# Fifteen weight slabs of block 2 split early and kept in DRAM as two parts, latent products among the gate products, full-height score products, and squares added on VectorE

## The chip, the cores and the metric

The kernel runs on one core of a Trainium2 chip. The metric is the device time of one execution in microseconds (us); lower is better. The core has five engines that run their own instruction queues in order: TensorE (PE, with its weight loads as PEld), VectorE (DVE), ScalarE (ACT), GpSimd (POOL) and SyncE (SP). SP issues most transfers; POOL issues some.

## The reference

1024 tokens of width 1024 pass through two blocks, in float32.

```python
# block 1
mod = silu(c) @ w_ada + b_ada                    # six vectors: shift, scale, gate, twice
h = rms_norm(x, g_pre_mix) * (1 + scale1) + shift1
xin, b_gate, c_gate, q, k, v, g = split(h @ w_in)            # 7 x 512 columns
y = concat(short_conv(xin, b_gate, c_gate), retention(q, k, v, g))
x = x + gate1 * rms_norm(y @ w_out, g_post_mix)
h = rms_norm(x, g_pre_mlp) * (1 + scale2) + shift2
x = x + gate2 * rms_norm(square(relu(h @ w_fc1)) @ w_fc2, g_post_mlp)
# block 2
a_q, a_k, a_v, i_q, i_k, i_w, c_q, c_kv, k_r, g = split(rmsnorm(x) @ w_in_2)
# indexer, 4 heads of 64: score = sum_h i_w * relu(i_q . i_k / 8); the top 256 keys of each query
# DSA: 8 heads of 64, one shared key/value head, attention over the selected keys, with a position bias
y_a = softmax(a_q . a_k / 8 + bias, over the selected keys) @ a_v
# MLA: latents c_q (256) and c_kv (128), each normalised and projected up; 8 heads of 64 + 32 (rotary)
y_b = softmax(causal (q_nope . k_nope + q_rope . k_rope) / sqrt(96)) @ v_b
gates = sigmoid(g + b_gate)                                   # 2 x 1024
x = x + (gates[0] * (y_a @ w_branch_a) + gates[1] * (y_b @ w_branch_b)) @ w_out_2
x = rmsnorm(x + square(relu(rmsnorm(x) @ w_ff1)) @ w_ff2, final_norm_g)
```

## The kernel before

**Precision.** Each float32 operand is held as two parts: a high part rounded to the short format that TensorE multiplies at full speed, and a low part, the rest. A product is three matmuls: high x high, high x low, low x high. A "unit" is one output tile of 128 features by 512 tokens (one half H of the tokens) over a contraction of 1024: 8 k-tiles x 3 = 24 matmuls of 128x512 (`unit`). Activations lie transposed, features on the partitions, so the weights are the stationary operand.

**Weights.** A `Stream` carries the weights in slabs of 128x1024 (512 KB). For each slab SP loads it into one of three raw tiles `wr`; ScalarE rounds it into the high tile `wh`; VectorE (or GpSimd, where `lo_engine` is set to it) subtracts to give the low tile `wl`. There are three split slots; `next()` hands out a slab and starts the split of slabs ahead. The list of slabs is written down in advance, in order of use, by `plan1` (block 1) and `plan2` (block 2).

**Order of work.** The main line issues units in a written order. Beside it, `Background` keeps lanes of generators (normalisations, retention steps, index scores, selection). A `tick` after each group of matmuls takes each lane one step on; a step yields a number of ticks to rest, a tuple of tiles that must have been written by a modelled clock (`Clock`), or "vector". The attention part is instead put in order by a planner (`Plan`) that knows a modelled cost for each step.

**Stages (us of the profiled execution).** Block 1's normalisation and first products to 195; the rest of its in-projection in four parts with the retention steps as a background lane, 195 to 427; out-projection of both halves (`out_proj`) 427 to 520; MLP up 520 to 857 (`up_first`, then `up_rest`), down to 1172. Block 2's projection: for each half of the tokens 12 units (`NZ` = 12: two of index queries, one `z2` with index keys, rotary keys and index weights, nine of gates), 1195 to 1365, with index scores beside them; then gate features m = 9 to 15 for both halves at once (1365 to 1446, 11.2 us each); then `bias_spread`, one transfer on POOL's queue that spreads the position-bias table within DRAM into `biasd` (4 MB); then six latent units (c_q twice, c_kv, for each half, 1446 to 1482) whose results are normalised by `latents` in the background; then ten units of DSA keys/values and queries. The selection of the top 256 (`top_k`) runs in the background on VectorE and ScalarE from 1340 to 1575. MLA follows to 1741, DSA to 1926, then the branches, `out2` and the second MLP.

**Slab order from the gates on (`plan2`).** Gate slabs m = 9 to 15 (seven), then three latent slabs twice (once for each half), then five key/query slabs twice: 23 loads and splits. From the second half's `z2` on `lo_engine` is GpSimd.

**Score products.** A query tile holds the high parts of 64 query features on partitions 0 to 63 and the low parts on 64 to 127. The key tile (`ik` for the indexer, `ak` for DSA) holds the high key parts on both halves of the partitions, and the low key parts on partitions 0 to 63 only, in further columns. One score tile is two matmuls: all 128 rows against the high keys, then 64 rows (high queries) against the low keys. DSA adds a mask matmul with the identity for query blocks from 2 on.

```python
nc.tensor.matmul(p[:, :w], self.iqs[:, s], self.ik[:, c0:c0 + w], start=True, stop=False)
nc.tensor.matmul(p[:, :w], self.iqs[0:64, s], self.ik[0:64, D + c0:D + c0 + w],
                 start=False, stop=True)
```

MLA's score products have 96 rows (64 + 32 features).

**Squares.** `sq_add` squares a tile on ScalarE and adds it to a running sum, on GpSimd unless another engine is given. `ada_chunks` streams the 12 column chunks of w_ada on POOL's queue in pairs of k-tiles and accumulates them on VectorE; it yields 3 ticks before it uses each.

Of the kernel before, what the change touches and what calls it, by code (L numbers as in the profile page):

```python
# [11 lines left out]
F32 = mybir.dt.float32  # L12
F32R = mybir.dt.float32r
BF16 = mybir.dt.bfloat16
I32 = mybir.dt.int32
AF = mybir.ActivationFunctionType
# [3 lines left out]
P = 128  # L20
T = 512
D = 1024
# [21 lines left out]
NZ = 12  # L44
# [299 lines left out]
class Stream:  # L344
# [42 lines left out]
    def add(self, width, pieces):  # L387
        x = {}

        def load():  # L390
            raw = x["raw"] = self.raw_tile()
            for dst, src in pieces:
                self.m.nc.sync.dma_start(dst(raw), src)

        after = self.ring("wr", self.RAW, len(self.entries))
        self.entry(self.parts_of(lambda: x["raw"][:, :width], width), load, after)

# [83 lines left out]
class Model:  # L481
# [321 lines left out]
    def ada_chunks(self, chunks, st):  # L803


        nc = self.nc
# [12 lines left out]
        for i, (c, k) in enumerate(todo):  # L819
            if k == 0:  # L820
                acc = self.t2()
            s = st[i % 2]
            yield 3
# [279 lines left out]
    def out_proj(self, x, nk=8):  # L1103

        f, acc = self.U(), self.acc_tile()
        for m in range(8):
            w = self.ws.next()
            p = self.ps()
            self.unit(p, w, x, nk)
            s = slice(m * T, m * T + T)  # L1110
            self.nc.scalar.activation(f[:, s], p, AF.Copy)
            self.sq_add(acc, f[:, s], m == 0)
        return f, acc
# [416 lines left out]
    def block1(self):  # L1530
# [109 lines left out]
        gD = bg.add(ada_rest(), lane=2)  # L1640
        ret = bg.add(self.retention(q, k, v))
# [9 lines left out]
        for part in range(4):  # L1651
# [5 lines left out]
            for m in range(4):  # L1657
                w = ws.next()
                p = self.pd()
                self.unit(p[:, 0], w, hA)  # L1660
                self.unit(p[:, 1], w, hB)
                pf = p.rearrange("p a b -> p (a b)")
# [14 lines left out]
                else:  # L1677
# [4 lines left out]
                    self.mix_part(mix[0], q, 1, m, 0)  # L1682
        bg.finish()
# [27 lines left out]
        bg.add(chain_b(f, acc))  # L1711
        self.up_first(hs[0])
# [192 lines left out]
    def plan2(self):  # L1905
# [3 lines left out]

# [14 lines left out]
        for m in range(NZ - 3, 16):  # L1924
            s.cols(w, GT + m * P)
        for cs in ((CQ, CQ + P, CKV), (AK, AQ, AQ + P, AQ + 2 * P, AQ + 3 * P)):
            for _ in range(2):
                for c in cs:
                    s.cols(w, c)
# [21 lines left out]
        self.plan_mlp(a["w_ff1_2"], a["w_ff2_2"])  # L1951

# [14 lines left out]
    def z_evac(self, kind, m, H, p):  # L1967
# [8 lines left out]
        elif kind == "z2":  # L1976
# [5 lines left out]
            nc.vector.tensor_sub(self.ik[0:64, lo], zr[0:64], self.ik[0:64, c].bitcast(F32))  # L1982
            return zr
# [51 lines left out]
    def index_scores(self, qbs, per=1):  # L2035
        nc = self.nc
        n_done = 0
        for qb in qbs:
            sc = self.score_tile(qb)
            n = P * (qb + 1)  # L2040
            for c0 in range(0, n, T):
                w = min(T, n - c0)
                for h in range(4):
# [3 lines left out]
                    nc.tensor.matmul(p[:, :w], self.iqs[0:64, s], self.ik[0:64, D + c0:D + c0 + w],  # L2047
                                     start=False, stop=True)
# [188 lines left out]
    def z_phase(self, xs, hs, f, acc, G2):  # L2237
# [19 lines left out]
        for H in range(2):  # L2257
            if H == 1:
                bg.finish(g0)
            for i in range(NZ):  # L2260
# [9 lines left out]
                if kind == "z2":  # L2270
# [9 lines left out]
                    else:  # L2280
# [10 lines left out]
                        bg.add(topk())  # L2291
        for m in range(NZ - 3, 16):
# [5 lines left out]
        bg.finish(scores)  # L2298
        self.bias_spread()
        self.lat = self.pair()  # L2300
        for H in range(2):
            raws = [self.t2(), self.t2()]
            raws.append(self.rope[:, 3 * D + H * T:3 * D + H * T + T])
            for m in range(3):
                w = ws.next()
                p = self.ps()
                self.unit(p, w, hs[H])
                nc.scalar.activation(raws[m], p, AF.Copy)
            bg.add(self.latents(raws, H), lane=1)
# [78 lines left out]
    def front(self, t, n, p, qb, marks):  # L2388
# [27 lines left out]
        a = step("PE", 1.3e-3 * w + 0.06, t, scores, self.inputs[n] + [self.last_a], takes=("pd",))  # L2416
# [141 lines left out]
    def qk_dsa(self, h, qb, lp):  # L2558
# [4 lines left out]
        for c0 in range(0, n, T):  # L2563
            w = min(T, n - c0)
            nc.tensor.matmul(lp[:, c0:c0 + w], q[:, qs], self.ak[:, c0:c0 + w], start=True, stop=False)
            nc.tensor.matmul(lp[:, c0:c0 + w], q[0:64, qs], self.ak[0:64, D + c0:D + c0 + w],
# [203 lines left out]
    def dsa_begin(self):  # L2770
# [20 lines left out]

        def turn():
# [18 lines left out]
        c = step("Pool", 2.4, t + 3, low, [b[0]])  # L2811
        d = step("PE", 0.6, t + 4, turn, [a], takes=("ps",))
# [88 lines left out]
    def out2(self, x, h, H):  # L2901
# [3 lines left out]
        for m in range(8):  # L2905
# [6 lines left out]
            self.sq_add(acc, x[:, s], m == 0)  # L2912
# [133 lines left out]
    def run(self):  # L3046
# [3 lines left out]
        self.xtokd = self.dp.tile([P, 2, 4 * D], F32, name="xtokd")  # L3050
        self.plan1()
# [38 lines left out]
```

## Time and profile before

| | us |
|---|---|
| median of 3 runs | 2787.26 (2783.12 to 2792.57) |
| profiled execution | 2785.2 |
| its span | 2783.4 |
| mean granted TensorE clock in it | 0.979 |
| TensorE busy | 2656.4 |
| VectorE busy | 1891.4 |
| ScalarE busy | 1334.7 |
| GpSimd busy | 439.1 |

The span is the time from the first to the last instruction that the profiler saw. Busy times are sums over an engine's instructions. Because one wrapper issues every instruction, all of them carry the same line, L183, and are told apart by the names of their tiles: `ps` and `pd` are PSUM tiles, `u` large activation tiles, `t` small ones, `wr`, `wh` and `wl` the raw, high and low weight tiles, `topk` the selection's. A line of the trace reads: engine, operation, output <- inputs, then shapes (for a matmul rows*columns of its stationary operand, then rows x columns of the moving one), type and count.

### The profile page before, as it was taken

The numbers are of one execution on the slowest core, as the hardware profiler recorded it, in microseconds if no ns is written. First come the engines' busy times: TensorE is split into PE (matmuls) and PEld (weight loads), VectorE is DVE, ScalarE is ACT, GpSimd is POOL, SyncE is SP. The second block draws the span as 40 slices with busy tenths as digits, with TensorE's granted clock in tenths as the row PEclk, the third lists the DMA queues.
The fourth block names the chain that finished last, engine by engine and source line by source line (L and its number), as shares of the span: only waits on it lengthen the run. The fifth ranks groups of instructions, "written<-read, shape, count | busy, mean of one in ns | idle before, by whom it ended". The sixth has DMA issues, their size and how long they took to land.

```text
span 2783.4 us, 33424 instructions
## 1 busy us (share of the span) xinstructions
PE 2656.4 (95%) x12052; PEld 2097.2 (75%) x12052; DVE 1891.4 (68%) x3155; ACT 1334.7 (48%) x2182; POOL 439.1 (16%) x384
## 2 busy tenths in 40 slices
PE   5999999999999999899998899999999999999987
PEld 4777777767888887776776678777887788888866
DVE  6573566777665567776898888786557466646656
ACT  4651114465444443444685477875135554443333
POOL 5040102300000110001223411420121000002012
PEclk7999999999999999999999999999999999999999
DMA  6542336454545896743334201453454564459773
GB/s 203 177 130 83 102 110 197 130 174 134 152 125 195 251 226 194 197 135 89 83 107 148 75 16 39 145 153 106 151 160 158 178 217 145 149 196 274 189 207 124
DMA packets 361708, 419.21 MB, mean 151 GB/s; under 512 B 33205, under 2 KB 265572, under 8 KB 360516
## 3 DMA queue, kind: packets, MB, share of 16 engines
q1 hardware_dynamic: 330664, 304.77, 35.4%
q0 software_dynamic: 30544, 112.14, 14.6%
q8 instruction: 95, 1.56, 0.2%
q14 instruction: 73, 0.60, 0.1%
q10 hardware_dynamic: 332, 0.14, 0.0%
HBM read 339.68 MB, written 80.45 MB: 151 GB/s over the span
## 4 chain that ended last, share of the span: by engine, by line
PE 61%; DVE 9%; ACT 6%; DMA 4%; issue 2%; POOL 0%; ACTq 0%; SPq 0%; POOLq 0%; DVEq 0%
PE ps L183 44%; PE pd L183 17%; DVE u L183 4%; ACT u L183 4%; DMA t<-opd 3%; DVE t L183 3%; ACT t L183 1%; DVE topk L183 1%; ACT wh L183 1%; DVE wl L183 1%; DVE tiny L183 1%; DMA opd<-t 0%; DMA wr<-in_w_in 0%; POOL wl L183 0%; POOL t L183 0%
## 5 line engine op out<-in xcount | busy, mean ns | idle before, releaser
L183 PE MATMUL ps<-u,wh 128*128 128x512 f32 (+1 forms) x3568 | 1146.8, 402 | 17.5 <-ACT wh L183 9.1
L183 PEld LDWEIGHTS ps<-u,wh 128*128 128x128 f32 (+1 forms) x3568 | 670.4, 190 | 189.5 <-ACT wh L183 13.1
L183 PE MATMUL ps<-u,wl 128*128 128x512 f32 (+1 forms) x1784 | 713.4, 400 | 7.6 <-DVE wl L183 5.9
L183 PE MATMUL pd<-u,wh 128*128 128x512 f32 x1600 | 521.5, 407 | 7.9 <-ACT u L183 5.5
L183 PEld LDWEIGHTS ps<-u,wl 128*128 128x128 f32 (+1 forms) x1784 | 339.1, 190 | 96.6 <-DVE wl L183 11.9
L183 DVE TENSOR_TENSOR wl<-wr,wh 128x1024 fp32r<-128x1024 f32 (+3 forms) x209 | 238.4, 1147 | 199.8 <-ACT wh L183 195.1
L183 PEld LDWEIGHTS pd<-u,wh 128*128 128x128 f32 x1600 | 299.0, 190 | 84.6 <-ACT u L183 6.4
L183 PE MATMUL pd<-u,wl 128*128 128x512 f32 x800 | 317.7, 397 | 0.0
L183 ACT ACTIVATE wh<-wr 128x1024 fp32r<-128x1024 f32 (+3 forms) x244 | 225.8, 931 | 177.7 <-PE pd L183 83.9
L183 ACT ACTIVATE t<-ps 128x512 f32<-128x512 f32 (+5 forms) x339 | 173.6, 522 | 237.5 <-PE ps L183 228.7
L183 DVE TENSOR_TENSOR t<-ps,t 128x384 fp32r<-128x384 f32 (+3 forms) x354 | 192.5, 563 | 91.8 <-PE ps L183 61.1
L183 ACT ACTIVATE u<-t 128x512 fp32r<-128x512 f32 (+4 forms) x174 | 145.2, 837 | 185.2 <-DVE t L183 117.2
L183 ACT ACTIVATE t<-t 128x512 f32<-128x512 f32 (+1 forms) x231 | 144.1, 625 | 94.1 <-DVE t L183 90.0
L183 DVE TENSOR_TENSOR u<-u 128x512 f32<-128x512 f32 (+3 forms) x144 | 145.1, 1011 | 63.9 <-ACT u L183 60.9
L183 ACT ACTIVATE wh<-u 128x1024 fp32r<-128x1024 f32 x96 | 101.2, 1055 | 172.1 <-PE ps L183 117.4
L183 PEld LDWEIGHTS pd<-u,wl 128*128 128x128 f32 x800 | 151.4, 189 | 37.0
L183 PE MATMUL pd<-wh,u 128*128 128x512 f32 x512 | 167.5, 406 | 10.8 <-ACT u L183 7.4
L183 DVE TENSOR_TENSOR wl<-u,wh 128x1024 fp32r<-128x1024 f32 x96 | 117.3, 1222 | 86.5 <-ACT wh L183 86.4
L183 DVE TENSOR_TENSOR u<-t,u 128x512 fp32r<-128x512 f32 (+3 forms) x145 | 134.1, 941 | 58.7 <-ACT u L183 58.5
L183 PE MATMUL ps<-wh,u 128*128 128x512 f32 (+1 forms) x576 | 173.7, 383 | 0.3 <-DVE u L183 0.3
L183 ACT ACTIVATE u<-ps 128x512 f32<-128x512 f32 (+2 forms) x171 | 95.9, 575 | 154.4 <-PE ps L183 149.2
L183 POOL DMA_DIRECT2D u<-opd x48 | 42.1, 1065 | 764.1 <-DMA u<-opd 639.9
(190 smaller groups left out, 3570.1 us busy)
## 6 DMA issues: line engine op xcount, KB each, us to landing
wr<-in_w_in SPq DMA_DIRECT2D x79, 512.0 KB, 4.1
wr<-in_w_fc SPq DMA_DIRECT2D x64, 512.0 KB, 4.6
opd<-t SPq DMA_DIRECT2D x128, 256.0 KB, 3.6
t<-opd SPq DMA_DIRECT2D x64, 512.0 KB, 4.7
wr<-in_w_ff SPq DMA_DIRECT2D x64, 512.0 KB, 4.1
u<-opd POOLq DMA_DIRECT2D x48, 512.0 KB, 11.2
u<-in_w_ada POOLq DMA_DIRECT2D x32, 512.0 KB, 4.3
wr<-in_w_out SPq DMA_DIRECT2D x32, 512.0 KB, 3.9
```

The lines of the kernel that those rows point to most:

```text
L183: return fn(*args, **kw)
```

## The change

Four edits.

1. *Slabs.* The 15 distinct slabs of the 23 loads named above get their own DRAM store `slabd`, high and low part side by side. `part_slabs`, in two background lanes (3 and 4) from the start of block 1's parts, takes 30 half slabs: an SP load of 256 KB into a `t4` tile, a ScalarE cast, a VectorE subtraction, and a POOL store of 512 KB (both parts of a half). The lanes are held from the end of part 1 to the end of the parts, with a half that is open by then stepped on at each unit pair, and must be done before `up_first`. In `plan2` the 23 entries become `parted` entries: two POOL loads of 512 KB straight into `wh` and `wl`, with no split. The adaLN chunks rest 2 ticks in place of 3.
2. *Order.* The slab order becomes two gates, latents, latents, five gates, keys and queries twice; the latent units run after gate m = 10 (`m == NZ - 2`); `bias_spread` stays behind the gate loop.
3. *Scores.* The low key parts are copied by ScalarE to partitions 64 to 127, and the second score product uses all 128 rows: the queries' low parts meet the keys' low parts too. In the planner a score column costs 1.37e-3 in place of 1.3e-3, and DSA's first stage gets a step `low_again`.
4. *Squares.* In block 1's `out_proj` and block 2's `out2` the squares are added on VectorE.

```diff
@@ line 397 @@
 
+    def parted(self, src, n):
+
+        def steps(hi, lo):
+            dma = self.m.nc.gpsimd.dma_start
+            return [lambda: dma(hi[:, :n], src[:, 1]), lambda: dma(lo[:, :n], src[:, 0])]
+        self.entry(steps)
+
     def cols(self, w, c0, n=P):
@@ line 822 @@
             s = st[i % 2]
-            yield 3
+            yield 2
             for e in range(2):
@@ line 1111 @@
             self.nc.scalar.activation(f[:, s], p, AF.Copy)
-            self.sq_add(acc, f[:, s], m == 0)
+            self.sq_add(acc, f[:, s], m == 0, self.nc.vector)
         return f, acc
@@ line 1640 @@
         gD = bg.add(ada_rest(), lane=2)
+        gS = [bg.add(self.part_slabs(e), lane=3 + e) for e in range(2)]
         ret = bg.add(self.retention(q, k, v))
@@ line 1660 @@
                 self.unit(p[:, 0], w, hA)
+                self.slabs_held |= part == 1 and m == 3
                 self.unit(p[:, 1], w, hB)
+                while part >= 2 and self.slabs_open:
+                    bg._step(3 + min(self.slabs_open))
                 pf = p.rearrange("p a b -> p (a b)")
@@ line 1682 @@
                     self.mix_part(mix[0], q, 1, m, 0)
+        self.slabs_held = False
         bg.finish()
@@ line 1711 @@
         bg.add(chain_b(f, acc))
+        for g in gS:
+            bg.finish(g)
         self.up_first(hs[0])
@@ line 1908 @@
         IQ, IK, IW, CQ, CKV, KR, AK, AQ, GT = 640, 896, 960, 964, 1220, 1348, 512, 0, 1380
-
         def z2():
@@ line 1923 @@
                 s.cols(w, GT + m * P)
-        for m in range(NZ - 3, 16):
-            s.cols(w, GT + m * P)
-        for cs in ((CQ, CQ + P, CKV), (AK, AQ, AQ + P, AQ + 2 * P, AQ + 3 * P)):
-            for _ in range(2):
-                for c in cs:
-                    s.cols(w, c)
+
+        gates = [GT + m * P for m in range(NZ - 3, 16)]
+        lat, rest = [CQ, CQ + P, CKV], [AK, AQ, AQ + P, AQ + 2 * P, AQ + 3 * P]
+        self.slabs = gates[:2] + lat + gates[2:] + rest
+        for cs in (gates[:2], lat, lat, gates[2:], rest, rest):
+            for c in cs:
+                s.parted(self.slabd[:, self.slabs.index(c)], D)
+        self.slabs = [w[:, c:c + P].rearrange("(k p) m -> p k m", p=P) for c in self.slabs]
         wq = a["w_uq_2"]
@@ line 1952 @@
 
+    def part_slabs(self, e):
+
+        nc = self.nc
+        halves = [(i, h) for i in range(len(self.slabs)) for h in range(2)]
+        self.slabs_held, self.slabs_open = False, set()
+        for i, h in halves[e::2]:
+            while self.slabs_held:
+                yield
+            self.slabs_open.add(e)
+            t = self.t4()
+            raw, hi = t[:, 0:T], t[:, T:2 * T]
+            nc.sync.dma_start(raw.rearrange("p (k m) -> p k m", k=4), self.slabs[i][:, 4 * h:4 * h + 4])
+            yield 3
+            nc.scalar.activation(hi.bitcast(F32R), raw, AF.Copy)
+            yield (hi,)
+            nc.vector.tensor_sub(raw.bitcast(F32R), raw, hi)
+            yield (raw,)
+            nc.gpsimd.dma_start(self.slabd[:, i, :, T * h:T * h + T], t.rearrange("p (s m) -> p s m", s=2))
+            self.slabs_open.discard(e)
+            yield
+
     def consts2(self):
@@ line 1982 @@
             nc.vector.tensor_sub(self.ik[0:64, lo], zr[0:64], self.ik[0:64, c].bitcast(F32))
+            nc.scalar.activation(self.ik[64:128, lo], self.ik[0:64, lo].bitcast(F32), AF.Copy)
             return zr
@@ line 2046 @@
                     nc.tensor.matmul(p[:, :w], self.iqs[:, s], self.ik[:, c0:c0 + w], start=True, stop=False)
-                    nc.tensor.matmul(p[:, :w], self.iqs[0:64, s], self.ik[0:64, D + c0:D + c0 + w],
-                                     start=False, stop=True)
+                    nc.tensor.matmul(p[:, :w], self.iqs[:, s], self.ik[:, D + c0:D + c0 + w], start=False, stop=True)
                     r = self.t2()
@@ line 2291 @@
                         bg.add(topk())
+        def latent_products():
+            bg.finish(scores)
+            self.lat = self.pair()
+            for H in range(2):
+                raws = [self.t2(), self.t2()]
+                raws.append(self.rope[:, 3 * D + H * T:3 * D + H * T + T])
+                for m in range(3):
+                    w = ws.next()
+                    p = self.ps()
+                    self.unit(p, w, hs[H])
+                    nc.scalar.activation(raws[m], p, AF.Copy)
+                bg.add(self.latents(raws, H), lane=1)
+
         for m in range(NZ - 3, 16):
@@ line 2297 @@
             self.g_pair(m, p)
-        bg.finish(scores)
+            if m == NZ - 2:
+                latent_products()
         self.bias_spread()
-        self.lat = self.pair()
-        for H in range(2):
-            raws = [self.t2(), self.t2()]
-            raws.append(self.rope[:, 3 * D + H * T:3 * D + H * T + T])
-            for m in range(3):
-                w = ws.next()
-                p = self.ps()
-                self.unit(p, w, hs[H])
-                nc.scalar.activation(raws[m], p, AF.Copy)
-            bg.add(self.latents(raws, H), lane=1)
         for H in range(2):
@@ line 2415 @@
         needs = [m["exp"] for m in marks]
-        a = step("PE", 1.3e-3 * w + 0.06, t, scores, self.inputs[n] + [self.last_a], takes=("pd",))
+        a = step("PE", 1.37e-3 * w + 0.06, t, scores, self.inputs[n] + [self.last_a], takes=("pd",))
         mla = n < 8
@@ line 2565 @@
             nc.tensor.matmul(lp[:, c0:c0 + w], q[:, qs], self.ak[:, c0:c0 + w], start=True, stop=False)
-            nc.tensor.matmul(lp[:, c0:c0 + w], q[0:64, qs], self.ak[0:64, D + c0:D + c0 + w],
+            nc.tensor.matmul(lp[:, c0:c0 + w], q[:, qs], self.ak[:, D + c0:D + c0 + w],
                              start=False, stop=qb < 2 and c0 + w < n)
@@ line 2791 @@
 
+        def low_again():
+            nc.scalar.activation(self.ak[64:128, D:2 * D], self.ak[0:64, D:2 * D].bitcast(F32), AF.Copy)
+
         def turn():
@@ line 2811 @@
         c = step("Pool", 2.4, t + 3, low, [b[0]])
+        c = step("ACT", 0.95, t + 5, low_again, [c])
         d = step("PE", 0.6, t + 4, turn, [a], takes=("ps",))
@@ line 2911 @@
             self.store_x(H, x, m)
-            self.sq_add(acc, x[:, s], m == 0)
+            self.sq_add(acc, x[:, s], m == 0, nc.vector)
         return acc
@@ line 3050 @@
         self.xtokd = self.dp.tile([P, 2, 4 * D], F32, name="xtokd")
+        self.slabd = self.dp.tile([P, 15, 2, D], F32, name="slabd")
         self.plan1()
```

## Rows read from the trace of the kernel before

**Rows 1.** The page, part 1: busy us, share of the span, instructions.
```profile
PE 2656.4 (95%) x12052; PEld 2097.2 (75%) x12052; DVE 1891.4 (68%) x3155; ACT 1334.7 (48%) x2182; POOL 439.1 (16%) x384
```

**Rows 2.** Windows: length, then busy us of PE, PEld, DVE, ACT, POOL; clock; DMA share.
```profile
195.00:427.00 232.00, 232.00 (x1043) 181.39 (x1042) 123.73 (x185) 38.69 (x52) 24.19 (x35) 1.00 0.35 106
427.00:520.00 93.00, 87.91 (x380) 69.85 (x379) 66.91 (x91) 42.16 (x62) 36.48 (x37) 0.98 0.59 187
1270.00:1345.00 75.00, 75.00 (x272) 47.70 (x271) 44.19 (x62) 36.39 (x63) 11.96 (x5) 1.00 0.28 74
1365.00:1577.00 212.00, 189.25 (x780) 149.13 (x778) 190.73 (x484) 137.19 (x240) 65.43 (x27) 0.94 0.40 114
1597.00:1741.00 144.00, 134.01 (x911) 113.81 (x912) 115.38 (x250) 107.29 (x234) 24.20 (x19) 0.98 0.08 27
1741.00:1920.00 179.00, 177.81 (x1138) 133.37 (x1136) 140.99 (x381) 135.47 (x301) 52.06 (x42) 1.00 0.47 143
```

**Rows 3.** Timeline of PE, index scores: start us, us, what; 4-matmul row is scores.
```profile
1304.26 0.63 PE L183 MATMUL ps<-u,wh 128*128 128x512 f32 x2
1304.73 0.39 PE L183 MATMUL ps<-u,wl 128*128 128x512 f32 x1
1304.96 1.67 PE L183 MATMUL ps<-u 128*128 128x512 f32 x4
1306.56 0.50 PE L183 MATMUL ps<-u,wh 128*128 128x512 f32 x1
```

**Rows 4.** Timeline of PE, DSA scores: a pair, then the mask product.
```profile
1802.76 0.91 PE L183 MATMUL pd<-u 128*128 128x512 f32 x2
1803.60 0.39 PE L183 MATMUL pd<-u,identb 128*128 128x512 bf16 x1
```

**Rows 5.** Timeline of PE, MLA scores.
```profile
1655.35 1.55 PE L183 MATMUL pd<-u 96*128 96x512 f32 x6
```

**Rows 6.** Groups by form on PEld, 1195 to 1345 and 1741 to 1920.
```profile
L183 PEld LDWEIGHTS ps<-u 64*128 64x128 f32 x40 | 7.3, 183 | 10.8 <-issue 10.2
...
L183 PEld LDWEIGHTS pd<-u 64*128 64x128 f32 x96 | 17.5, 183 | 21.1 <-issue 19.6
```

**Rows 7.** Waits of DVE, 1741 to 1920: us in total, times, longest.
```profile
DVE t L183 <- ACT t L183: 19.2, 33, 1.3
```

**Rows 8.** Waits of PE, 1440 to 1600.
```profile
PE ps L183 <- DVE tiny L183: 9.7, 3, 5.3
PE ps L183 <- DVE t L183: 8.1, 3, 5.9
```

**Rows 9.** Groups by form, 1340 to 1577: busy, mean ns | idle before.
```profile
L183 POOL TENSOR_TENSOR wl<-wr,wh 128x1024 fp32r<-128x1024 f32 x27 | 67.6, 2504 | 160.8 <-ACT wh L183 149.1 <-PE ps L183 11.6
L183 ACT ACTIVATE wh<-wr 128x1024 fp32r<-128x1024 f32 x28 | 29.4, 1048 | 0.0
...
L183 DVE TENSOR_SCALAR topk<-topk 128x3 int32<-128x3 int32 x62 | 20.0, 322 | 0.1
...
L183 DVE SCALAR_TENSOR_TENSOR topk<-topk 128x3 int32<-128x3 int32 x63 | 7.4, 159 | 0.0
```

**Rows 10.** Transfers of the span: queue, count, KB each, median us to landing.
```profile
wr<-in_w_in SPq DMA_DIRECT2D x79, 512.0 KB, 4.1
u<-in_w_ada POOLq DMA_DIRECT2D x32, 512.0 KB, 4.3
...
biasd<-tab POOLq DMA_DIRECT2D x1, 4096.0 KB, 27.8
```

**Rows 11.** Tile wr, 1449 to 1476: its four loads.
```profile
DMA to landing us min/median/max: 12.4/14.1/15.8
```

**Rows 12.** Groups by form on DVE, whole span.
```profile
L183 DVE TENSOR_TENSOR t<-t,t 128x512 f32<-128x512 f32 x61 | 43.5, 715 | 9.8 <-ACT t L183 8.3
```

**Rows 13.** Waits of PE, 427 to 520.
```profile
PE ps L183 <- POOL t L183: 3.7, 1, 3.7
```

## Prediction

> **What bounds the kernel now.** I read the busy times first: TensorE is busy 95% of the span, VectorE 68%, ScalarE 48% [rows 1]. So only two things can pay much: columns that TensorE no longer streams, and the few stretches where it waits. The windows by stage show which is which [rows 2]. In block 1's projection (195 to 427 us) TensorE has no gap at all, while ScalarE works 39 us and VectorE 124 us of 232. The stretch with the index scores (1270 to 1345) is TensorE's alone, 75 of 75 us. The stretch of the top-256 selection (1365 to 1577) is the poor one: TensorE is busy 189 of 212 us at a granted clock of 0.94, VectorE 191. In MLA attention TensorE works 134 of 144 us, in DSA attention 178 of 179.
>
> **128-row scores.** A plain 128x512 product follows the next at 0.233 us: three in 0.70 us, from 1304.26 to 1304.96 [rows 3]. Then come four score products, two score pairs of one 128-row and one 64-row product each, and they take 1.60 us (1304.96 to 1306.56): 0.40 each in place of 0.233. The page shows the same in DSA: a score pair from 1802.76 to 1803.60, 0.84 us for two products and no more [rows 4]. MLA's products have 96 rows all the time, and six take 1.55 us with the drain of the last, 0.26 each at most [rows 5]. So a row count under 128 costs nothing by itself; it is the switch between 128 and 64 rows, pair by pair, that costs about 0.17 us at each change. The edit makes both products of a pair 128 rows deep (the low keys are copied to rows 64 to 127; the query's tile already holds its high and low halves on the two), and so no switch is left. The weight loads of 64 rows are 40 and 96 in number [rows 6], one for each pair.
>
> The Trainium skill, "TensorE: Matmul & The Clock Gate", section "LDWEIGHTS (loading the stationary operand)", speaks against this edit: a weight load costs by its columns, and 32 rows load as fast as 128. By it, doubling the rows would win nothing, and 32 us of the sum below would fall out. The alternating pairs at 0.40 us against at most 0.26 at 96 rows say that something beyond that rule is paid here.
>
> Index scores: 40 pairs x (0.80 - 0.467) = 13 us, and TensorE is the only bound there, so -13 (bounds -15, and 0 if the cost is not the switch). DSA: 48 pairs are 512 wide, 0.84 - 0.466 = 0.37 us each; the 48 narrower ones aren't timed apart, I take 0.33 each; together 33 us. TensorE's 177.8 us would become 145. But then VectorE is late next: 141.0 us of work [rows 2], and 19.2 us in which it waits on ScalarE's exponentials [rows 7], 160 in all. A faster TensorE removes none of the latter by itself. I take 179 to 160, -19 (bounds -33, if those waits close up as well, and 0). The planner's cost of a score column rises from 1.3e-3 to 1.37e-3; it decides only the order of steps. MLA has 10 us of TensorE's idle time to give or lose by that: 0, bounds ±5. ScalarE's extra copies (0.6 twice, 1.05 once) lie beside 135 of 179 and 36 of 75 busy microseconds: nothing, or 2 us uncovered.
>
> **Parted slabs and the order of products.** From 1365 to 1577 TensorE runs seven gate pairs, six latent units and ten of keys and queries: 30 x 24 = 720 products, 168 us at 0.233; some 60 others are about 13 us more. It needs 181 of the 212 us. It idles 23 us, 17.8 of them on the latents' norms (9.7 and 8.1 us, VectorE) [rows 8] and the rest mostly on the split of the next slab; the other 8 us go to the clock of 0.94. Latents moved ahead of the last five gate pairs have 5 x 11.2 = 56 us in which their norms can end, so those two waits go. Splitting goes too: 23 ScalarE casts of 1.05 us and 23 GpSimd subtractions of 2.50 us, of the 28 and 27 in the view [rows 9]. VectorE's selection steps show two prices in that view, 0.322 us for the tensor-scalar step and 0.159 for the next, of the same shape; 62 x 0.163 = 10 us is what GpSimd's neighbourhood can account for there, and I take up to twice this over all selection steps. TensorE then sets the end again: 181 + 3 = 184 us, -28.
>
> Something new is late: the slabs now come by GpSimd's queue, and in it the bias-table spread stands ahead of the later ones. This copy moves 4 MB and takes 27.8 us to land [rows 10]. Weight loads issued while it runs take 12.4 to 15.8 us [rows 11], against the usual 4.1. GpSimd, which has no split to wait for now, issues the spread once its slot is free, some 11 us before the first product of the last group. So it ends about 17 us into that group; the third slab's two 512 KB parts, queued behind it, land near 21 us, and are wanted at 11.2. So a stall of some 10 us, which comes once: the ring is deep again after it. Net -18. Bounds: -30 if the spread shares the queue without harm, -8 if the stall is double, with half of the rest.
>
> The Trainium skill, "SBUF — State Buffer", section "Who interferes with whom", adds that GpSimd writes the descriptors of its own transfers and can be locked out while VectorE is in a two-port mode; its remedy is another engine's queue. By it every parted slab could be late under the selection. The 32 loads of the adaLN weights on GpSimd's queue land after 4.3 us beside VectorE's work [rows 10], hardly later than SyncE's 4.1; no row shows it beside the selection.
>
> **The slab parting in block 1.** 30 half slabs, each a 256 KB load on SyncE's queue, a cast on ScalarE (0.63 us, half of 1.05 and its fixed part), a subtraction on VectorE (0.715, the price of its 128x512 subtraction) [rows 12], and a 512 KB store on GpSimd's queue. In all 19 us of ScalarE and 21 of VectorE over 195 to 640, where these have 193 and 108 us to spare in the first window alone [rows 2]: nothing on the path. What can be late is a matter of order. Two lanes share a ring of two tiles; a load that waits for the last store of its tile (4.1 to 4.3, the price of a 512 KB load [rows 10]) and lands somewhat under 4.1 later is near 8 us away, while five ticks cover 7 to 9 (1.4 to 1.8 us each). If it is late, the cast stands in ScalarE's queue ahead of a retention step or an eviction. I take 0.6 us x some 13 halves, of which not all reach TensorE, and the 30 loads ahead of weight loads in SyncE's queue, which runs three raw and three split slabs ahead (16.8 us): +3 in sum. The adaLN chunks, one tick shorter each, only end sooner.
>
> **Squares on VectorE.** 14 additions in the out-projection move from GpSimd to VectorE (0.715 each [rows 12]), where VectorE works 67 of 93 us [rows 2]. The wait of 3.7 us on GpSimd's last addition [rows 13] goes: -3. In block 2's out-projection the same move: 0, ±2. Block 1 as a whole: 0, bounds ±8 (+8 if each half costs TensorE a quarter microsecond).
>
> **Sum.** -13 - 19 - 18 + 3 - 3 = -50, on the profiled execution's 2785.2 us (span 2783.4, and 1.8 around it): 2735. The median of the runs is 2787.3, 2 us more, so I say 2736.
>
> **Rivals.**
> *DSA passes wholly to VectorE and ScalarE.* They are busy 141 and 135 of 179 us and hand each tile on to one another; if their chain, not TensorE, already paces the stage, 33 us of columns buy 4. For it: 19.2 us of VectorE idle on ScalarE. Against: TensorE is busy 177.8 of the 179 us and waits for nobody. -35: 2751.
> *The selection stretch gains nothing.* The spread and its 12 to 16 us loads, or late parts of each slab (reads double to 1 MB per 5.6 us unit, 187 GB/s, as much as 427 to 520 shows [rows 2]), eat all of it: 2754.
> *Better than forecast.* DSA gives the whole 33 and the selection 28 to 30: 2710.
> *The rows are not the cause.* The pairs cost 0.40 us a product for another reason, and the score edits do nothing: only the selection's 18 is left, 2767. (The Trainium skill's section on LDWEIGHTS, above, stands on this side.)
> *Slower.* The parting holds ScalarE's or VectorE's in-order queue in 195 to 640 us: each half waits for its load there, and retention and evictions, and with them TensorE, wait behind. Thirty halves must cost TensorE 1.9 us each, 58 us, to pass the gain of 50 and reach 8 us beyond: above 2795. Against it: the casts are released by the modelled clock and five ticks.
>
> **How the numbers follow.** The forecast 0.60, its own range 2722 to 2748; DSA's bound 0.14; the selection's 0.10; better 0.08; rows not the cause 0.04; slower 0.04. A measurement of this kernel can tell about 0.3% (8 us) from no change. The range 2712 to 2762 takes in the first three and most of the unknown prices; it leaves out some 2 in 10 (slower, rows, the better half of the best case, and ends of the others). Of the rows' case and the selection's a quarter may, with a dear block 1, end within 8 us of before: same 0.03, slower 0.04, faster 0.93.
>
> **What would show it.** The score pairs should start 0.47 us apart and the forms with 64 rows be gone; if they still take 0.8, the row step is wrong. DSA should last about 160 us with VectorE and ScalarE near 0.88 and 0.85 of it; if it stays at 175 they paced it. From 1365 the waits on the latents' norms should be gone, 23 casts and 23 subtractions fewer, and one wait of about 10 us on a slab's transfer stand behind the spread; more such waits would show GpSimd's queue to be the new bound. TensorE should stay without gaps from 195 to 427; gaps there on ScalarE or VectorE would show the parting's price, and so would a wait on GpSimd that survives in 427 to 520. I'd be wrong most if the score pairs keep their price or the slabs come late throughout.

## The result and the profile after

The changed kernel takes 2748.5 us (median; 2745.3 to 2750.6) against 2787.0 for the kernel before in the same comparison: 0.986 of it, 95% interval 0.984 to 0.988. That is 38.5 us less where 50 were forecast, inside the range. It lies at the far end of the forecast's own range (2722 to 2748) and nearer to the 2751 of the rival on DSA, so the total doesn't tell these two apart; the stages, e1 and e9 below do. The profiled execution took 2745.3 us (span 2743.6), 39.9 less than the one of before.

Both kernels issue 12,052 weight loads, so one such load (by its number in order) marks the same place in both traces. The lengths between such marks show where the time went. The places are us of the changed kernel; the forecast stands beside them.

| stretch | change, us | forecast |
|---|---|---|
| 250 to 427, block 1's projection | +4.1 | +3 (all parting) |
| 427 to 515, out-projections | -3.2 | -3 |
| 515 to 640, first MLP products | +5.3 | 0 |
| 1270 to 1335, index scores | -15.2 | -13 |
| 1355 to 1550, selection | -17.9 | -18 |
| 1569 to 1712, MLA | -1.7 | 0 |
| 1712 to 1889, DSA | -7.9 | -19 |
| 2660 to 2743, the end | -3.0 | 0 |

The last line is no merit of the edit: nothing there was changed, and the granted clock was 0.95 in place of 0.91 (first before, then after):

```profile
2700.00:2783.00 83.00, 65.31 (x270) 51.02 (x268) 58.94 (x102) 34.12 (x51) 22.57 (x15) 0.91 0.41 127
2660.00:2743.00 83.00, 67.51 (x284) 52.56 (x282) 58.34 (x103) 34.36 (x52) 22.57 (x15) 0.95 0.44 133
```

The rest makes about -37. MLA's -1.7 can't be told from chance: in e11, which leaves MLA as it is, down to the order of its products, it is 3.7 us longer than in the changed kernel.

The windows of the changed kernel for these stretches (length, busy us of PE, PEld, DVE, ACT, POOL; clock, DMA share, GB/s) answer to [rows 2]:

```profile
195.00:431.00 236.00, 232.65 (x1041) 181.78 (x1041) 141.81 (x216) 48.48 (x69) 39.52 (x56) 0.99 0.56 170
520.00:570.00 50.00, 39.77 (x154) 29.26 (x153) 41.35 (x73) 29.17 (x45) 8.39 (x10) 0.90 0.53 173
1270.00:1335.00 65.00, 65.00 (x296) 52.18 (x295) 46.14 (x64) 35.78 (x65) 12.03 (x5) 1.00 0.38 93
1355.00:1550.00 195.00, 182.39 (x781) 145.69 (x780) 162.77 (x486) 116.11 (x218) 30.75 (x47) 0.96 0.56 178
1712.00:1889.00 177.00, 164.29 (x1159) 134.43 (x1172) 144.04 (x389) 138.37 (x307) 51.28 (x41) 0.98 0.49 150
```

The index stretch is TensorE's from end to end, as before, only shorter. In DSA TensorE now idles 13 of 177 us. In the selection VectorE has lost 28 us of work, from 190.7 to 162.8.

**Scores.** The timeline of TensorE shows a score pair, then the next product, and in DSA the six products of two 512-wide chunks:

```profile
1296.67 0.62 PE L183 MATMUL ps<-u 128*128 128x512 f32 x2
1297.14 0.63 PE L183 MATMUL ps<-u,wh 128*128 128x512 f32 x2
...
1793.76 0.71 PE L183 MATMUL pd<-u 128*128 128x512 f32 x2
1794.31 0.39 PE L183 MATMUL pd<-u,identb 128*128 128x512 bf16 x1
1794.35 0.81 PE L183 MATMUL pd<-u 128*128 128x512 f32 x2
1795.01 0.39 PE L183 MATMUL pd<-u,identb 128*128 128x512 bf16 x1
```

An index pair takes 0.47 us in place of 0.80 [rows 3]; the six DSA products 1.64 us, from 1793.76 to 1795.40.

**Selection.** The waits of TensorE on the latents' norms [rows 8] are gone, and one wait stands in their place: 10.3 us on a slab. GpSimd's timeline shows the spread, and behind it the next two slab loads. The landing times are those of the eight slab transfers from 1455 to 1500. The groups by form are VectorE's selection steps, which answer to [rows 9]:

```profile
PE ps L183 <- DMA wh<-slabd: 10.3, 1, 10.3
```
```profile
1465.47 1.12 POOL L183 DMA_DIRECT2D biasd<-tab  x1
1475.62 0.55 POOL L183 DMA_DIRECT2D wh<-slabd  x1 [9.03 <-PE pd L183]
1476.16 0.54 POOL L183 DMA_DIRECT2D wl<-slabd  x1
```
```profile
DMA to landing us min/median/max: 4.5/17.2/22.1
```
```profile
L183 DVE TENSOR_SCALAR topk<-topk 128x3 int32<-128x3 int32 x57 | 9.7, 169 | 0.0
L183 DVE SCALAR_TENSOR_TENSOR topk<-topk 128x3 int32<-128x3 int32 x59 | 7.0, 160 | 0.0
```

The spread is issued at 1465.5; slabs issued 10 us later land up to 22 us after their issue. The tensor-scalar step falls from 322 to 169 ns, while the step beside it in [rows 9] stays where it was (159, now 160). The 322 is a mean of two kinds: between 1365 and 1577 of the kernel before, nine of the 57 tensor-scalar steps take 0.4 to 2.4 us, each of them beside a GpSimd instruction, and the others 0.17. None of the 59 steps of the other kind ran beside one, so their steady price doesn't tell whether they would be held up too.

**Block 1.** Near 300 us the parting does what the prediction's slower rival described, once. The rows are from the timelines of SyncE, ScalarE, VectorE and TensorE; brackets give the idle time before an instruction and what ended it:

```profile
290.23 3.90 SPq L183 DMA_DIRECT2D t<-in_w_in  x2
...
296.19 0.63 ACT L183 ACTIVATE t<-t 128x512 fp32r<-128x512 f32 x1 [17.59 <-DMA t<-in_w_in]
...
297.81 1.23 DVE L183 TENSOR_TENSOR wl<-wr,wh 128x1024 fp32r<-128x1024 f32 x1 [7.17 <-ACT wh L183]
...
301.14 0.69 PE L183 MATMUL ps<-ident,t 128*128 128x128 f32 x2 [3.35 <-DVE t L183]
```

SyncE's second half-slab load waited for the last store of its tile. ScalarE stood at that half's cast, with the next weight's cast behind it; VectorE waited for the weight, with the adaLN sum behind it; TensorE waited 3.35 us for the sum. Near 525 TensorE waits again:

```profile
PE ps L183 <- POOL t L183: 4.9, 1, 4.9
PE ps L183 <- ACT u L183: 3.8, 2, 3.1
```

### The profile page after: what moved, and what is told of

The parts are those of the page before. It is cut to its first block, busy times and chain, and to the rows that moved or that the text cites. A ratio compares the mean times of both kernels' runs of the same rounds, so it can differ in the third digit from the quotient of the medians.

```text
span 2743.6 us, 33563 instructions
## 1 busy us (share of the span) xinstructions
PE 2610.7 (95%) x12037; PEld 2086.5 (76%) x12052; DVE 1881.1 (69%) x3213; ACT 1331.3 (49%) x2192; POOL 391.8 (14%) x409
## 5 line engine op out<-in xcount | busy, mean ns | idle before, releaser
L183 PE MATMUL ps<-u,wh 128*128 128x512 f32 (+1 forms) x3568 | 1138.2, 400 | 27.5 <-DMA wh<-slabd 10.3
L183 PEld LDWEIGHTS ps<-u,wl 128*128 128x128 f32 (+1 forms) x1784 | 336.8, 189 | 95.8 <-DVE wl L183 13.4
L183 DVE TENSOR_TENSOR wl<-wr,wh 128x1024 fp32r<-128x1024 f32 (+3 forms) x209 | 223.8, 1077 | 180.5 <-ACT wh L183 176.8
L183 ACT ACTIVATE wh<-wr 128x1024 fp32r<-128x1024 f32 (+3 forms) x221 | 201.9, 920 | 167.4 <-PE pd L183 74.7
L183 ACT ACTIVATE t<-t 128x512 f32<-128x512 f32 (+2 forms) x261 | 163.1, 627 | 160.6 <-DVE t L183 89.1
L183 ACT ACTIVATE u<-u,topk 128x768 bf16<-128x768 f32 (+8 forms) x157 | 135.0, 860 | 34.2 <-DVE topk L183 32.3
```

The source lines that it names most:

```text
L183: return fn(*args, **kw)
```

## The experiments

Each is an edit of the changed kernel. Ratios are to the kernel before, timed on the same chip; the changed kernel's is 0.986 (0.984 to 0.988). Intervals are some 0.002 either way, 5 us, so smaller effects are read from the traces, stretch by stretch, between the same weight loads as above. Those have noise of their own: in the runs whose edit is elsewhere DSA stays within 1.0 us of the changed kernel, 515 to 550 within 1.4, and MLA moves by up to 4.

**Rows.** `e1` puts the 64-row products back; `e2` also sends DSA's products by kind.

```diff
-  matmul(p, self.iqs[:, s], self.ik[:, D + c0:...])        # and the same in qk_dsa
+  matmul(p, self.iqs[0:64, s], self.ik[0:64, D + c0:...])
```
```diff
-  for each chunk: 128-row product, 64-row product, mask    # qk_dsa, e2
+  128-row products of all chunks; 64-row products of all; masks of all
```

(e2's lines give the order in words.)

> The changed kernel with the second score product at 64 rows again, for the index scores and for DSA; the copies to partitions 64 to 127 stay. Theory (a switch between 128 and 64 rows costs some 0.17 us, and DSA was cut short by VectorE's chain): the index stretch gives back the 13 to 15 us that it won, DSA only 8 to 10, so about 23 us over the changed kernel, near 2771. Rival (the row count is not the cause, the gain in these stretches came from the order of work): within 5 us of the changed kernel. Rival (DSA also won by the planner's new cost): less than 5 us back in DSA.

Measured: 2775.3 us, ratio 0.996 (0.994 to 0.997). The index stretch is 15.2 us longer, exactly as before. DSA is 16.3 us longer, more than expected, and 8 longer than in the kernel before, with the same products. What else differs there is the planner's cost, ScalarE's one copy of the low keys (1 us), and VectorE's waits on bias loads, 6.0 us where they were 1.7; e1 doesn't tell these apart.

> As e1, but DSA's products of one tile are sent by kind: both 128-row products of a 1024-wide tile, then both 64-row products, then the masks. Theory (the switch is what costs): the second 128-row and the second 64-row product run at about 0.23 us start to start, so a tile over 512 wide costs two switches in place of four, 0.34 us less; DSA some 3 to 8 us shorter than in e1. Rival (a 64-row product is dear in itself, wherever it stands): both 64-row products stay near 0.5 us, and DSA stays as in e1.

Measured: 2766.9 us, ratio 0.993 (0.991 to 0.994); DSA is 7.3 us over the changed kernel, 9.0 less than in e1. The six products of two chunks, first in the kernel before (the two rows that follow [rows 4]), then in e2:

```profile
1803.63 1.01 PE L183 MATMUL pd<-u 128*128 128x512 f32 x2
1804.58 0.39 PE L183 MATMUL pd<-u,identb 128*128 128x512 bf16 x1
```
```profile
1791.02 1.37 PE L183 MATMUL pd<-u 128*128 128x512 f32 x4
1792.32 0.60 PE L183 MATMUL pd<-u,identb 128*128 128x512 bf16 x2
```

Before, 1802.76 to 1804.97, 2.21 us with four switches (128 to 64 and back, twice). In e2, 1791.02 to 1792.92, 1.90 us with two. Changed kernel, 1.64 with none. (2.21 - 1.64) / 4 = 0.14 and (1.90 - 1.64) / 2 = 0.13 us a switch: in sum the cost goes by the switches, not by the two 64-row products, which are in both. In e2 the starts of the two 64-row products are still some 0.33 us apart in the trace, not the expected 0.23, so the total is shown and its place within the group is not. DSA has 32 tiles wider than 512, and 32 x 0.31 = 10 us is close to the 9.0, a little over the 3 to 8 expected.

**The spread.** `e3` issues it before the second half's units; `e4` leaves it in place, on SyncE's queue.

```diff
   if H == 1:
       bg.finish(g0)
+      self.bias_spread()                       # e3; taken out behind the gate loop
```
```diff
-  self.nc.gpsimd.dma_start(dst, src)           # bias_spread, e4
+  self.nc.sync.dma_start(dst, src)
```

> The changed kernel with the 4 MB bias-table spread issued before the second half's twelve units, some 190 us earlier. Theory (the one 10.3 us wait of TensorE on a slab comes from the spread): that wait goes, 8 to 10 us less than the changed kernel, near 2739. Rival (the slabs are late by the 1 MB per unit itself, or descriptors are starved under the selection): the wait stays within 3 us of 10. A third way: the spread in its new place makes the weight loads there 12 to 16 us late, and TensorE waits there instead.

Measured: 2748.7 us, ratio 0.986 (0.985 to 0.988), no gain. The old wait is gone (-12.4 us between 1457 and 1500), and the third way took it all back: +15.5 us between 1270 and 1335. The weight loads there, from 1255 to 1300 (first the time that SyncE's issues took, in ns), and the clock tell it:

```profile
L183 SPq DMA_DIRECT2D wr<-in_w_in x6: 367/373/10079, 1257.9 to 1289.2; - x6
DMA to landing us min/median/max: 3.9/13.4/23.0
```
```profile
1270.00:1290.00 20.00, 11.82 (x35) 7.83 (x34) 10.33 (x16) 8.40 (x13) 0.00 (x0) 0.70 0.64 191
1290.00:1310.00 20.00, 20.00 (x79) 15.60 (x79) 10.86 (x16) 9.51 (x15) 0.00 (x0) 0.88 0.34 92
```

The trace tells the landing of only two of the six, so the 13.4 is no typical value: 23.0 us for the load issued at 1258.3, beside the copy (issued at 1248.5, landed 31.9 us later), and 3.9 for one issued after it. A load just ahead of this window, at 1251.8, took 17.8. So on SyncE's queue, far from GpSimd's, these two loads landed 18 and 23 us after their issue beside the copy, and two of SyncE's issues took 10.1 and 9.2 us themselves, where 0.37 is usual. TensorE idles 8 of 20 us, and the granted clock is 0.70 and then 0.88.

> The changed kernel with the spread at its place, but on SyncE's queue. Theory (the slab stands behind the spread in GpSimd's queue, in order): the wait falls to a few us, 5 to 10 us less than the changed kernel. Rival (the copy takes the transfer engines from whoever loads, whatever the queue): each slab's 1 MB takes 12 us and more while the copy runs, and the wait stays at 8 us or more, spread over several slabs.

Measured: 2739.4 us, ratio 0.983 (0.982 to 0.985). Between 1457 and 1500 it is 12.4 us shorter, 1.7 come back by 1550. The twelve slab transfers from 1455 to 1500 land so:

```profile
DMA to landing us min/median/max: 4.2/7.3/9.6
```

So both mechanisms are real. The copy slows what runs beside it (the ten parts issued beside it land after 6.9 to 9.6 us, where the medians of all 23 slabs in the changed kernel are 4.2 for the high parts and 5.5 for the low ones), which three slots absorb; it was the place behind it in one queue (15.3 to 22.1) that made TensorE wait. Why loads on SyncE's queue took longer beside the copy (12.4 and 15.8 us in [rows 11], where the trace knows two landings of the four, and 17.8 and 23.0 in e3) than slabs on GpSimd's do here is not shown.

**Block 1.** `e5` rests 8 ticks, not 3, between a half's load and its cast. `e6` leaves the five key and query slabs whole (20 halves in place of 30). `e7` puts the squares back on GpSimd. `e11` forces the lanes to their end behind the first MLP products.

```diff
-      yield 3                                  # part_slabs, after the load
+      yield 8                                  # e5
...
-  self.slabs = gates[:2] + lat + gates[2:] + rest
+  self.slabs = gates[:2] + lat + gates[2:]     # e6; the rest by s.cols(w, c)
...
-  self.sq_add(acc, f[:, s], m == 0, self.nc.vector)
+  self.sq_add(acc, f[:, s], m == 0)            # e7; the same in out2
...
-  for g in gS: bg.finish(g)                    # e11: moved
   self.up_first(hs[0])
   bg.finish()
+  for g in gS: bg.finish(g)
```

> The changed kernel with a rest of 8 ticks in place of 3 between a half slab's load and its cast. Theory (block 1 lost 4 us near 300 and 8 near 525 because ScalarE stood at a cast whose load waited for the last store of its tile): the wait of 3.4 us near 300 goes and part of the loss near 525, 4 to 8 us less; against it, more halves are left to be forced through at the end of the second out-projection, which could cost as much there. Rival (the loss is VectorE's and ScalarE's added work, not waiting): no change in either place.

Measured: 2797.9 us, ratio 1.005 (1.003 to 1.007), slower than before. The first half of the theory held: 4.9 us less between 250 and 320, all that the parting cost there. The second failed in size: 56 us more between 515 and 550, in one wait.

```profile
PE ps L183 <- ACT u L183: 64.1, 1, 64.1
```

A dozen halves were left, and were forced through one after the other, each cast at its load, with the first MLP products' input behind them on ScalarE. This is the slower rival at full size.

> The changed kernel with the five key and query slabs, used twice each, left whole: loaded by SyncE and split by ScalarE and GpSimd at use as before, so 20 half slabs in block 1 in place of 30. Theory: parting ends before the second out-projection's end, and the 8 us near 525 go; in the selection stretch the 10.3 us wait behind the spread goes, but ten splits by GpSimd come back beside the selection (25 us of its work, VectorE dearer beside it), and loads take 12 to 16 us beside the copy against a lead of 16.8: 5 to 15 us less than the changed kernel. Rival (parting the rest is what made room in the selection): the stretch loses 10 us or more and the sum is no change or slower.

Measured: 2744.7 us, ratio 0.986 (0.984 to 0.988), the same as the changed kernel. The parting ends at 464 us, and the 515 to 550 stretch is 11.2 us shorter. Between 1457 and 1500 another 11.9 are saved. But the selection now ends 18.1 us later against that, and TensorE waits for it in one piece:

```profile
PE ps L183 <- DVE t L183: 18.3, 1, 18.3
```
```profile
1346.00:1546.00 200.00, 179.26 (x783) 143.58 (x782) 185.22 (x486) 125.09 (x228) 51.95 (x39) 0.96 0.47 145
L183 DVE TENSOR_SCALAR topk<-topk 128x3 int32<-128x3 int32 x57 | 12.5, 218 | 0.0
```

Ten GpSimd splits come back, VectorE is busy 185 of 200 us there (its tensor-scalar step at 218 ns), and its chain sets the end.

> The changed kernel with the squares of both out-projections added on GpSimd again. Theory (the wait of 3.7 us on GpSimd's last addition between the halves): 3 to 5 us slower, in the first out-projection's end alone, nothing in block 2's. Rival (GpSimd's stores of the parted slabs now stand between the additions): more, 6 us and above. Rival (no part of the 5 us won there is due to it): no change.

Measured: 2749.9 us, ratio 0.989 (0.987 to 0.991). 2.8 us more between 470 and 515 and 2.5 between 515 and 550, 5.3 together; nothing in block 2. TensorE's wait on GpSimd's last addition grows from 4.9 us to this:

```profile
PE ps L183 <- POOL t L183: 6.9, 1, 6.9
```

> The changed kernel with the lanes of half slabs forced to their end behind the first MLA products in place of ahead of them. Theory (what costs 8 us near 525 is the forced end: ScalarE and VectorE emptied for the last halves, each cast at its load, with the first MLA products' split and norm behind them): 5 to 9 us less than the changed kernel, in that place. Rival (the casts that the ticks bring in the last units of the out-projection cost it, before any forcing): less than 3 us.

("MLA products" there are the first MLP products.)

Measured: 2747.3 us, ratio 0.986 (0.985 to 0.988). 1.7 us less between 515 and 570, hardly more than runs show there whose edit is elsewhere; the waits are 4.3 and 3.8 where they were 4.9 and 3.8. So the rival holds: in the changed kernel the forced end is not what costs.

**Queue of the bias loads.** `e8` loads the first six branch slabs by GpSimd.

```diff
-  s.add(D, pieces)
+  s.add(D, pieces, self.nc.gpsimd if m < 6 else None)
```

> The changed kernel with the first six branch weight slabs loaded by GpSimd's queue in place of SyncE's. Theory (in DSA the bias loads stand in SyncE's queue behind a branch load that waits for its raw tile; VectorE's 7.3 us of waits on bias loads, 5.0 in one piece, come from there): those waits fall under 2 us and DSA is 3 to 6 us shorter. Rival (the bias loads are late because of the traffic, not the queue): the waits stay. Rival (VectorE and ScalarE pace DSA in any case): the waits go and DSA stays within 2 us.

Measured: 2743.5 us, ratio 0.986 (0.984 to 0.987). VectorE's waits on bias loads in DSA (in the kernel before, the changed one and e8):

```profile
DVE u L183 <- DMA u<-biasd: 1.7, 3, 0.8
DVE u L183 <- DMA u<-biasd: 7.3, 3, 5.0
DVE u L183 <- DMA u<-biasd: 1.5, 2, 1.0
```

DSA is 3.4 us shorter by the trace, less than the 5.8 us of waits that went; the timed ratio doesn't tell it from the changed kernel (MLA was 3.7 longer in the profiled execution).

**The planner's cost.** `e9` takes back one number.

```diff
-  a = step("PE", 1.37e-3 * w + 0.06, ...)
+  a = step("PE", 1.3e-3 * w + 0.06, ...)
```

> The changed kernel with the planner's old cost of a score column, 1.3e-3, and nothing else. The run with 64-row products (e1) had DSA 16 us longer than the changed kernel, where the kernel before is only 9 longer. Theory (the new cost gives away some 7 us by the order that it makes): DSA 3 to 8 us shorter than in the changed kernel. Rival (with 128 rows VectorE and ScalarE pace DSA, and the order matters little; the cost fits the new price of a product): within 2 us, or longer by some us.

Measured: 2737.8 us, ratio 0.982 (0.980 to 0.983). DSA is 5.6 us shorter. The medians differ by 10.7, over two comparisons, and e12 against e4, the same number taken back, differs by 10.7 too. Only the part in DSA is placed: the number changes the order of steps in MLA as well, but there the trace shows no gain (2.2 us longer, within that stage's noise). Its window and VectorE's waits in it:

```profile
1716.00:1888.00 172.00, 163.19 (x1177) 135.46 (x1176) 143.59 (x390) 138.68 (x309) 51.56 (x41) 0.99 0.49 155
```
```profile
DVE t L183 <- ACT t L183: 15.7, 29, 1.4
DVE u L183 <- DMA u<-biasd: 4.8, 2, 3.0
```

**Combinations.** `e10` is e4 with 13 slabs parted (26 halves); `e12` is e4 with e9's number.

> The changed kernel with the spread on SyncE's queue, as in e4, and only 13 slabs parted: the last two query slabs, used twice each, stay whole, so 26 half slabs in block 1 in place of 30, and four splits come back in the selection stretch. Theory: the loss near 525 us goes as in e6 (-8 to -11), the wait behind the spread goes as in e4 (-11), and four splits in place of e6's ten cost 2 to 7 us: 2728 to 2738. Rival (the split slabs are late beside the copy however few they are): e6's 18 us come back in good part, and it ends above 2742.

Measured: 2749.8 us, ratio 0.986 (0.985 to 0.988); the rival. Four splits beside the selection put its end some 11 us behind e4's, where e6's ten cost 18, and TensorE waits for it:

```profile
PE ps L183 <- DVE t L183: 13.0, 1, 13.0
```

With 26 halves nothing is won near 525, though the last of them is stored at 512.

> The changed kernel with the spread on SyncE's queue (e4) and the planner's old cost (e9). Theory (the two losses lie in stages that don't touch, 1450 to 1550 us and DSA): they add, 9 and 6 to 11 us less than the changed kernel, 2728 to 2734. Rival (SyncE's queue, with the copy in it, holds back the loads that MLA and DSA need, so that the better order finds its inputs late): no better than the better of the two, about 2738.

Measured: 2728.7 us, ratio 0.981 (0.979 to 0.982): the best kernel here, 20 us under the changed one by the medians. In the trace the parts add: -12.4 us behind the spread, -6.7 in DSA. Its ratio's interval overlaps e9's and, barely, e4's.

## Why the prediction was right, and which terms were not

**Index scores: right.** -15.2 for -13, on a stretch where TensorE was and is the only bound. That is 0.38 us a pair where one pair of [rows 3] gave 0.33, and e1, which puts the 64 rows back, loses exactly these 15.2 us.

**The switch: right, and what was drawn from the rule against it fell.** Row, group and stretch all go by the switches: 0.13 to 0.14 us each in DSA, 0.17 to 0.19 in the index scores (half of 0.33 and 0.38). The Trainium skill's "TensorE: Matmul & The Clock Gate", section "LDWEIGHTS (loading the stationary operand)", by which the row count should not matter, holds for rows that stay equal [rows 5]; it says nothing of a change of row count, and the runs decide here.

**DSA: right in kind, wrong in size.** The term -19 measured -7.9. In the window of [rows 2] that is 179 to 171, nearer to the 175 that was to show the rival (VectorE and ScalarE pace DSA) than to 160. Yet the rows by themselves gave 16.3 us (e1), although a pair gave back 0.29 us (0.57 for two) where the prediction had 0.37: it took 0.466 for a plain pair, and here a pair takes 0.55 and 0.66 up to its mask product (the rows under Scores). Two things stood against it that I had set to nothing. The step "it decides only the order of steps ... 0" failed: the new cost took back 5.6 us of DSA by the trace (e9; 6.7 in e12 against e4). And VectorE, next in line as forecast, got a new wait: bias loads behind branch slabs in SyncE's queue, 7.3 us where it was 1.7 before; e8 shows the queue as the cause, and that it cost DSA 3.4 us. With the old cost alone the edit gives 7.9 + 5.6 = 13.5 us, so the rival's 4 us were wrong too. That VectorE's and ScalarE's chain paces the rest fits the traces of the changed kernel and of e9 (144 us of work, 16 to 18 of waits on ScalarE, 5 to 7 on bias loads, in 177 and 172 us), but no run made that work shorter, so it is argued, not shown.

**Selection: right in sum and in parts.** The norms' waits went, the forecast stall of some 10 us came at the forecast place, the third slab of the last group, and measured 10.3, and VectorE lost 28 us of work where I took up to 20. What I had not written is how near VectorE was to setting the end: e6 and e10 show that a few splits beside the selection make TensorE wait 13 to 18 us for its end. The Trainium skill, "SBUF — State Buffer", section "Who interferes with whom", lists tensor-scalar operations among those that can contend with GpSimd; the trace agrees: nine steps stood beside GpSimd's work for 0.4 to 2.4 us, and the mean of all such steps goes from 322 ns to 218 with twelve splits left (e6) and to 169 with two. Its warning on transfers issued by GpSimd did not come true: the high parts' 23 loads land after a median of 4.2 us beside the selection, and only the three behind the copy take over 5.1.

**Parting in block 1: the rival in small.** The +3 of the sum measured +4.1 in the first window, by the very chain of the slower rival (e5 removes it), so "not all reach TensorE" was right there. The failed part is the stretch near 525, which I had covered with spare engine time: parting beside the second out-projection costs 11 us there (e6), the squares give back 5 (e7, forecast 3). Not the forced end (e11), and not the last four halves alone (e10). So the six halves that are stored between 464 us, where e6 ends, and 512, where e10 does, are enough for the loss. Which of ScalarE's, VectorE's and GpSimd's turns in the norm of the first half carries it stays open. Block 1 as a whole came to +6 (4.1 - 3.2 + 5.3) where 0 was forecast, inside its bounds of ±8.

## What to carry to other kernels

Count switches of a matmul's row count, not only its columns: filling the short operand up to the full height (here with the low parts, which are of use; zero rows were not tried) can be cheaper than being short. When a stage's bound moves from one engine to the next, price the planner's numbers and the next engine's queues too, because a cost that only sets an order took back 5.6 us of DSA by the trace, 10.7 by the medians, beside 38.5 that the edit won. Work put into idle time costs by its place in each in-order queue, not by its busy time: some 19 us of ScalarE's work between 195 and 640 us cost TensorE 4 us in one place, 11 in another, and 56 more when it was forced (e5).

## What the runs showed of the hardware

A change between 128 and 64 rows from one matmul to the next cost 0.13 to 0.14 us in DSA and 0.17 to 0.19 in the index scores; six products of 96 rows in a row start 0.23 us apart, as those of 128 rows do ([rows 5], [rows 3]). A 4 MB copy within DRAM on GpSimd's queue made loads on SyncE's land after 17.8 and 23.0 us (e3) where 4.1 is usual; beside the copy on SyncE's queue, slabs on GpSimd's landed after 6.9 to 9.6 (e4); behind it in the same queue they landed after 15.3 to 22.1. A wait of TensorE can cost more than its length: in e3 it idled 8 us, the granted clock fell to 0.70 and 0.88, and the stretch lost 15.5.
